# The conv branch's input projection as 2x2 block products: seven products of half size in place of eight, in two groups of 1024 tokens

## Chip, core and metric

The kernel runs on one core of a Trainium2 chip. The metric is device microseconds of one execution. In three runs the kernel before took 3139.97, 3140.99 and 3141.83 us, median 3140.99 us.

## What is computed

A two-layer decoder trunk on 2048 tokens of width 1024, in float32. The layer that the change touches projects the normed input to eight parts, runs retention on four of them and a gated short convolution on the other four, and projects both results back:

```python
q, k, v, g_ret, cb, cc, cx, g_conv = split_cols(h @ w_in, EVEN_SPLITS)
...
y_conv = cb * short_conv(cc * cx, conv_w, conv_b)
mix = jnp.concatenate([r * jax.nn.silu(g_ret), y_conv * jax.nn.silu(g_conv)], axis=-1)
return mix @ w_out
```

`cb`, `cc`, `cx` and `g_conv` are each 2048 tokens by 1024 channels, so the conv branch's input projection is 1024 x 4096 weights against 1024 x 2048 inputs. The convolution has three taps along the tokens. The second layer (latent attention) is not touched.

## The kernel before

**Numbers.** PE multiplies in fp32r. Each float32 operand is kept as a high part (a ScalarE copy) and a low part (VectorE: source less high part), by `split` (L72 to 74), and each product is three matmuls, high x high, high x low, low x high (`mm3`, L76 to 79). The transposed input lies in `uTH[tb]`, `uTL[tb]`, four blocks of 512 tokens.

**Retention (L284 to 498).** 64 units (8 heads, 8 pairs of 128 tokens) run as a software pipeline in which step `s` projects unit `s` on PE (48 matmuls), rotates and gates it (`post`), and finishes units `s-1` to `s-3`. PE passes through these pieces in the order in which they are written; so does every other engine through its own. Three more steps drain the pipeline; in them PE already runs the first convolution product (`conv_mm(0, ...)`, L478), while GpSimd, VectorE and ScalarE finish the last units.

**Convolution (L500 to 535).** For each of 8 blocks of 128 channels the parts cx, cc, g_conv, cb follow each other. One part is 128 channels x 2048 tokens: two calls of `conv_mm`, each 2 x 8 x 3 = 48 matmuls of 128x128 against 128x512 into a PSUM tile of two banks (tag `proj`, two buffers), 3072 matmuls in all. Behind PE each bank is read once: cx is copied by ScalarE, cc multiplied by VectorE, then two taps by VectorE, and so on. Weights come as raw pieces by SyncE's queue and are split by `piece_split`, 64 pieces.

**Order and memory.** Nothing schedules: the order is that of the code, engine by engine, and a semaphore stands where one engine needs another's result. Tiles come from pools, and a new tile in a place waits for every reader and writer of the tile before it there; dependences are followed by tile (`reuse_waits="tile"`), so two banks in one tile count as one. The weight tiles are a ring of three (tag `w`, L172). The output side (L537 on) opens new pools over the same memory; its first three weight tiles (`worw`, L616) lie where the third tile of that ring lay.

## Time and profile before

| | |
|---|---|
| median of 3 runs | 3140.99 us |
| span of the profiled execution | 3139.9 us |
| retention and everything ahead of it | 0 to 719.6 us |
| convolution products on PE | 719.6 to 1420.4 us |
| output side and second layer | 1421.8 us on |
| busy share: PE, VectorE, ScalarE, GpSimd | 99%, 43%, 32%, 17% |

The page covers one execution; its own time is its span, 3139.9 us, from the first instruction to the last, and what lies around it in a run is the 1.1 us to the median. A matmul's listed duration (389 ns in the convolution) is its way through the array and overlaps with the next one's, so rates are read from counts in a stretch, not from durations.

### The profile page before, as it was taken

How to read it: one execution, taken by the hardware profiler on the slowest of the kernel's cores; microseconds unless marked ns; L12 is line 12 of the kernel's file. 1: busy time of each engine (PE TensorE's matmuls, PEld its weight loads, DVE VectorE, ACT ScalarE, POOL GpSimd, SP SyncE). 2: the span in 40 equal slices, each digit the busy share in tenths (PEclk: the TensorE clock that was granted, in tenths of full speed). 3: DMA queues.
4: the chain of work that ended last, by engine and by line, in shares of the span. 5: the costliest groups of instructions: out<-in, count | busy, mean ns of one | idle time of the engine just before them, and what ended most of it. 6: DMA issues, size and time to landing. Idle time of an engine off the chain costs nothing.

```text
span 3139.9 us, 44468 instructions
## 1 busy us (share of the span) xinstructions
PE 3105.7 (99%) x17169; PEld 2739.2 (87%) x17169; DVE 1361.8 (43%) x3102; ACT 996.3 (32%) x2593; POOL 547.7 (17%) x941
## 2 busy tenths in 40 slices
PE   7999999999999999999999999999999999999998
PEld 7999999998888888888888888998899999999887
DVE  6533333332211222225323311568666666666643
ACT  5322122211111111114222321343555555555521
POOL 2111111110000000000111101014333333333210
PEclk9999999999999999999999999999999999999999
DMA  4210111001111111116333532325312211112552
GB/s 137 63 32 29 35 35 31 25 31 31 37 38 37 41 38 37 30 38 210 121 118 111 176 126 78 115 91 214 109 61 63 71 51 60 58 57 62 170 164 85
DMA packets 226325, 244.64 MB, mean 78 GB/s; under 512 B 33841, under 2 KB 189121, under 8 KB 226113
## 3 DMA queue, kind: packets, MB, share of 16 engines
q1 hardware_dynamic: 201360, 158.13, 16.9%
q0 software_dynamic: 24432, 83.38, 7.1%
q8 instruction: 135, 2.21, 0.3%
q14 instruction: 78, 0.63, 0.1%
q10 hardware_dynamic: 320, 0.29, 0.0%
HBM read 157.86 MB, written 83.89 MB: 77 GB/s over the span
## 4 chain that ended last, share of the span: by engine, by line
PE 97%; DVE 1%; DMA 1%; ACT 1%; issue 0%; SPq 0%; POOL 0%; DVEq 0%; POOLq 0%; ACTq 0%
PE y L582 11%; PE cv L77 7%; PE cv L79 7%; PE cv L78 7%; PE pj L77 6%; PE pj L79 6%; PE pj L78 6%; PE fy L1354 5%; PE T L1159 4%; PE o L1189 2%; PE o L1188 2%; PE o L1187 2%; PE S L1106 2%; PE S L1109 2%; PE S L1110 2%; PE S L1107 2%
## 5 line engine op out<-in xcount | busy, mean ns | idle before, releaser
L77 PE MATMUL cv<-uTH,w_c 128*128 128x512 f32 x1024 | 398.6, 389 | 1.4 <-ACT p L517 1.4
L79 PE MATMUL cv<-uTH,w_c 128*128 128x512 f32 x1024 | 398.4, 389 | 0.0
L78 PE MATMUL cv<-uTL,w_c 128*128 128x512 f32 x1024 | 398.4, 389 | 0.0
L77 PE MATMUL pj<-w_r,uTH 128*128 128x384 f32 x896 | 310.5, 346 | 0.0
L79 PE MATMUL pj<-w_r,uTL 128*128 128x384 f32 x896 | 299.9, 335 | 0.0
L78 PE MATMUL pj<-w_r,uTH 128*128 128x384 f32 x896 | 299.6, 334 | 0.0
L1127 POOL TENSOR_SCALAR P<-P,al 128x512 f32<-128x512 f32 (+2 forms) x320 | 218.7, 694 | 354.5 <-DVE al L1132 169.4
L1117 ACT ACTIVATE P<-S,nm 128x512 f32<-128x512 f32 (+2 forms) x320 | 200.8, 628 | 197.7 <-DVE nm L1114 172.4
L77 PEld LDWEIGHTS cv<-uTH,w_c 128*128 128x128 f32 x1024 | 192.2, 188 | 41.5 <-ACT p L517 1.7
L79 PEld LDWEIGHTS cv<-uTH,w_c 128*128 128x128 f32 x1024 | 192.2, 188 | 40.0
L78 PEld LDWEIGHTS cv<-uTL,w_c 128*128 128x128 f32 x1024 | 192.2, 188 | 39.8
L1114 DVE TENSOR_REDUCE nm<-S 128x1 f32<-128x512 f32 (+2 forms) x320 | 194.4, 609 | 71.3 <-PE S L1110 43.1
L1187 PE MATMUL o<-TH,vH 128*128 128x256 f32 x576 | 185.2, 322 | 0.0
L1163 DVE TENSOR_TENSOR TL<-T,TH 128x512 fp32r<-128x512 f32 x224 | 154.3, 689 | 63.3 <-ACT TH L1162 62.0
L77 PEld LDWEIGHTS pj<-w_r,uTH 128*128 128x128 f32 x896 | 168.3, 188 | 9.6 <-issue 9.6
L78 PEld LDWEIGHTS pj<-w_r,uTH 128*128 128x128 f32 x896 | 168.5, 188 | 0.0
L79 PEld LDWEIGHTS pj<-w_r,uTL 128*128 128x128 f32 x896 | 168.2, 188 | 0.0
L1159 PE MATMUL T<-ident,P 128*128 128x128 f32 x1088 | 166.2, 273 | 0.0
L1189 PE MATMUL o<-TH,vL 128*128 128x256 f32 x576 | 162.9, 283 | 0.0
L1188 PE MATMUL o<-TL,vH 128*128 128x256 f32 x576 | 162.2, 282 | 0.0
L582 PE MATMUL y<-woH,mH 128*128 128x512 f32 x512 | 159.0, 392 | 1.4 <-ACT woH L73 1.4
L582 PE MATMUL y<-woH,mL 128*128 128x512 f32 x512 | 157.7, 389 | 0.1
(310 smaller groups left out, 6691.6 us busy)
## 6 DMA issues: line engine op xcount, KB each, us to landing
raw<-in_even_w_in SPq DMA_DIRECT2D x94, 256.0 KB, 3.0
qn_d<-qn POOLq DMA_DIRECT2D x32, 512.0 KB, 3.1
aqn<-qn_d SPq DMA_DIRECT2D x64, 256.0 KB, 3.2
mr<-mix_d SPq DMA_DIRECT2D x56, 256.0 KB, 2.8
mix_d<-mxo POOLq DMA_DIRECT2D x32, 256.0 KB, 2.7
mix_d<-a POOLq DMA_DIRECT2D x16, 512.0 KB, 3.5
worw<-in_even_w_out SPq DMA_DIRECT2D x16, 512.0 KB, 5.0
xr<-in_x SPq DMA_DIRECT2D x16, 512.0 KB, 4.0
```

The source lines that it names most:

```text
L77: PE.matmul(o, ah, bh, start=first, stop=False)
L78: PE.matmul(o, ah, bl, start=False, stop=False)
L79: PE.matmul(o, al, bh, start=False, stop=last)
L582: PE.matmul(ys[t][i], a, w[k][:, i * 512:(i + 1) * 512], start=first and pi == 0, stop=last and pi == 2)
L1114: V.reduce_max(nm[:, j:j + 1], sp[:, 0:w], axis=AX.X, negate=True)
L1117: later(D_EXP, lambda: A.activation(p_[:, 0:w], sp[:, 0:w], AF.Exp, bias=nm[:, j:j + 1], accum_out=sm[:, j:j + 1]))
L1127: G.tensor_scalar(t_[:, 0:ww], t_[:, 0:ww], al[:, jj:jj + 1] if n > 1 else al[:, 5:6], al[:, 5:6] if n > 1 else 1.0, op0=ALU.mult, op1=ALU ...
L1159: PE.transpose(tp[:, e, z, :], src, ident)
L1187: PE.matmul(hold[i], vH[h][:, kb, :], pth[:, c], start=first, stop=False)
L1188: PE.matmul(hold[i], vH[h][:, kb, :], ptl[:, c], start=False, stop=False)
L1189: PE.matmul(hold[i], vL[h][:, kb, :], pth[:, c], start=False, stop=last)
L1354: PE.matmul(y[i], a[:, k, :], w[k][:, i * 512:(i + 1) * 512], start=k == 0 and pi == 0, stop=k == KT - 1 and pi == 2)
```

## The change

The conv projection is taken as a 2x2 block product. A *quad* is one block of 128 channels in two of the four parts (even quads: cx and cc; odd quads: g_conv and cb), both halves of the 1024 input rows (4 weight blocks A11, A12, A21, A22, each 512 rows by 128 channels), and two token blocks of 512 (4 input blocks B11 to B22). There are 32 quads: two groups of 1024 tokens, in each 8 channel blocks, in each an even and an odd quad. In place of eight block products a quad has seven, of 12 matmuls each, in the order A11, S2, S1, S3, A22, A12, S4; S1 to S4 are sums and differences of weight blocks, and each is multiplied by its partner B11, T2, T1, T3, T4, B21, B22, where T1 to T4 are sums and differences of input blocks. The four results are put together from PSUM by further sums: `p1_copy` (ScalarE copies the A11 product), `u2_`, `u3`, `c22`, `c21`, `c12` (VectorE). S3 adds onto the bank of S2, A12 onto that of A11, S4 onto that of S1, so each of these has to wait until VectorE or ScalarE has read what stood there.

The T blocks are made once by GpSimd during retention (`comb_ops`, three instructions a step from step 10 on, 108 additions of 128x512), written to memory, and read back and split when their group needs them (`u_dma`, `u_split_`). The S blocks are made by GpSimd per quad (`w_step`, 5 additions of 128x512), and all seven weight blocks are split per quad, one quad ahead of PE; as each weight block is used in both groups, its data is loaded and split twice. Products A11, S2, S1 of the first quad fill the drain of retention. What follows the sums (`finish`) is put off until after the next quad's first product. The vector `gnb` gives way to one per head, and its place is used for sums (`tc`).

```diff
+    uc_d = dram.tile([2, 7, P, 4, 512], F32, name="uc_d")
...
+        ORDER = ("A11", "S2", "S1", "S3", "A22", "A12", "S4")
+        UOF = dict(zip(ORDER, ("B11", "T2", "T1", "T3", "T4", "B21", "B22")))
+        UIX = {n_: i for i, n_ in enumerate(("B11", "T2", "T1", "T3", "T4", "B21", "B22"))}
+        BANK = dict(zip(ORDER, (0, 1, 2, 1, 3, 0, 2)))
+        QUADS = [(g, ct, w) for g in range(2) for ct in range(8) for w in range(2)]
+        COFF = ((OCX, OCC), (OGC, OCB))
...
+        def w_step():
+            n_ = wcnt["prep"]
+            q, j = divmod(n_, 7)
+            if q >= len(QUADS):
+                return
+            wcnt["prep"] += 1
+            i = ORDER[j]
+            r = qraw[q]
+            f = lambda t: t.rearrange("p k c -> p (k c)")
+            if j == 0:
+                r["s"] = base.tile([P, 2, 4, P], F32, tag="tc", bufs=1, name=f"s12_{q}")
+                r["S1"], r["S2"] = r["s"][:, 0], r["s"][:, 1]
+                G.tensor_tensor(out=r["S1"], in0=r["A21"], in1=r["A22"], op=ALU.add)
+                G.tensor_tensor(out=r["S2"], in0=r["S1"], in1=r["A11"], op=ALU.subtract)
+            elif j == 3:
+                r["s"] = base.tile([P, 2, 4, P], F32, tag="tc", bufs=1, name=f"s34_{q}")
+                r["S3"], r["S4"] = r["s"][:, 0], r["s"][:, 1]
+                G.tensor_tensor(out=r["S3"], in0=r["A11"], in1=r["A21"], op=ALU.subtract)
+                G.tensor_tensor(out=r["S4"], in0=r["A12"], in1=r["A22"], op=ALU.subtract)
+                G.tensor_tensor(out=r["S4"], in0=r["S4"], in1=r["S3"], op=ALU.add)
+            if n_ % 3 == 0:
+                wring.append(w_tile(f"wq{n_}"))
+            t = wring[-1][:, (n_ % 3) * 1024:(n_ % 3 + 1) * 1024].rearrange("p (z k c) -> p z k c", z=2, k=4)
+            split(t[:, 0], t[:, 1], r[i])
+            qtile[q, i] = t
+            if j == 5:
+                raw_dma()
+        def banks(q):
+            if q not in bks:
+                if q % 2 == 0:
+                    t_ = [psb.tile([P, 2, 512], F32, tag="proj", bufs=2, name=f"qb{q}_{i}") for i in range(2)]
+                    bks[q] = [t_[0][:, 0, :], t_[1][:, 0, :], t_[0][:, 1, :], t_[1][:, 1, :]]
+                else:
+                    bks[q] = [psb.tile([P, 512], F32, tag=tg, bufs=1, name=f"qb{q}_{tg}") for tg in ("tr", "m", "sc", "r")]
+            return bks[q]
+        def p1_copy(q):
+            p1[q] = base.tile([P, 512], F32, tag="p1", bufs=1, name=f"p1_{q}")
+            A.copy(p1[q], banks(q)[0])
+        def product(q, i):
+            b = BANK[i]
+            o = banks(q)[b]
+            W, (UH, UL) = qtile.pop((q, i)), ucs[QUADS[q][0]][UOF[i]]
+            for k in range(4):
+                first = k == 0 and i in ("A11", "S2", "S1", "A22")
+                mm3(o, W[:, 0, k, :], W[:, 1, k, :], UH[:, k, :], UL[:, k, :], first, k == 3, i in ("A12", "S3", "S4"))
+        def u_dma(g, n_, tag, where=None):
+            if where is None:
+                t = base.tile([P, 2, 4, 512], F32R, tag=tag, name=f"uc{g}_{n_}")
+                where = (t[:, 0], t[:, 1])
+            ucs[g][n_] = where
+            SP.dma_start(f32(where[1]), uc_d[g, UIX[n_]])
+        def u_split_(g, n_):
+            H, L = ucs[g][n_]
+            for c in (slice(0, 2), slice(2, 4)):
+                A.copy(H[:, c], f32(L)[:, c])
+                V.tensor_tensor(out=L[:, c], in0=f32(L)[:, c], in1=f32(H)[:, c], op=ALU.subtract)
+        UTAG = {"T2": "uTH2", "T1": "uTL2", "T3": "uTH3", "T4": "uTL3", "B21": "uTH0", "B22": "uTL0"}
...
+        NG = len(QUADS) // 2
+        USPLIT = {(NG - 1, 0): "B11", (NG - 1, 5): "T2", (NG - 1, 6): "T1", (NG, 1): "T3", (NG, 2): "T4", (NG, 3): "B21", (NG, 4): "B22"}
...
+                    def first(H=H, L=L, g=g, k=k):
+                        t = base.tile([P, 2, 512], F32, tag="tc", bufs=1, name=f"tc12_{g}{k}")
+                        c0, c1 = t[:, 0], t[:, 1]
+                        yield lambda: sub(c0, H("B12"), H("B11"))
+                        yield lambda: sub(c1, L("B12"), L("B11"))
+                        yield lambda: add(c0, c0, c1)
+                        yield lambda: sub(c1, H("B22"), c0)
+                        yield lambda: add(c1, c1, L("B22"))
+                        yield lambda: (put("T1", c0), put("T2", c1))
...
-                if n <= s < n + 2:
-                    conv_mm(0, s - n)
+                if s == n:
+                    product(0, "A11")
+                    product(0, "S2")
+                elif s == n + 1:
+                    p1_copy(0)
+                    product(0, "S1")
...
+                if s > 9:
+                    for _ in range(3):
+                        f_ = next(tops, None)
+                        if f_ is not None:
+                            f_()
+                if s == n - 7:
+                    raw_dma()
+                for _ in range({n - 6: 1, n - 5: 1, n - 4: 1, n: 2, n + 1: 2}.get(s, 0)):
+                    w_step()
+                if s == n - 3:
+                    u_dma(0, "T2", UTAG["T2"])
+                    u_dma(0, "T1", UTAG["T1"])
...
+                elif s == n - 2:
+                    u_split_(0, "T2")
+                elif s == n - 1:
+                    u_split_(0, "T1")
+                    u_dma(0, "T3", UTAG["T3"])
+                    u_dma(0, "T4", UTAG["T4"])
+                elif s == n + 1:
+                    u_split_(0, "T3")
+                elif s == n + 2:
+                    u_split_(0, "T4")
...
+            for q, (g, ct, w) in enumerate(QUADS):
...
+                for j, i in enumerate(ORDER):
+                    if q > 0 or i not in done0:
+                        product(q, i)
+                    if last:
+                        u_next(j)
+                    if j == 0:
+                        flush()
+                    elif j == 1:
+                        if q > 0:
+                            p1_copy(q)
+                    elif j == 2:
+                        u2_ = cp.tile([P, 512], F32, tag="u2", bufs=1, name=f"u2_{q}")
+                        V.tensor_tensor(out=u2_, in0=x_, in1=p1[q], op=ALU.add)
+                    elif j == 4:
+                        u3 = p1.pop(q)
+                        V.tensor_tensor(out=u3, in0=x_, in1=u3, op=ALU.add)
+                        c22 = cp.tile([P, 512], F32, tag="c", bufs=4, name=f"c22_{q}")
+                        V.tensor_tensor(out=c22, in0=y_, in1=u3, op=ALU.add)
+                    elif j == 5:
+                        c21 = cp.tile([P, 512], F32, tag="c", bufs=4, name=f"c21_{q}")
+                        V.tensor_tensor(out=c21, in0=u3, in1=z_, op=ALU.subtract)
+                    w_step()
+                    if (q, j) in USPLIT:
+                        u_split_(1, USPLIT[q, j])
+                def finish(q=q, g=g, ct=ct, w=w, a=a, y_=y_, u2_=u2_, c21=c21, c22=c22, pv=pv, av=av):
+                    c12 = cp.tile([P, 512], F32, tag="c", bufs=4, name=f"c12_{q}")
+                    if w == 0:
+                        V.tensor_tensor(out=pv[:, 2:514], in0=a, in1=c21, op=ALU.mult)
+                        V.tensor_tensor(out=c12, in0=y_, in1=u2_, op=ALU.add)
+                        G.tensor_copy(pv[:, 0:2], halo[:, ct, :])
+                        V.tensor_tensor(out=pv[:, 514:1026], in0=c12, in1=c22, op=ALU.mult)
+                        for o in (0, 512):
                             A.activation(av[:, o:o + 512], pv[:, 2 + o:2 + o + 512], AF.Identity, scale=convw[:, 2, ct:ct + 1],
                                          bias=convb[:, ct:ct + 1])
+                        for o in (0, 512):
                             for tap in (1, 0):
                                 V.scalar_tensor_tensor(out=av[:, o:o + 512], in0=pv[:, tap + o:tap + o + 512],
                                                        scalar=convw[:, tap, ct:ct + 1], in1=av[:, o:o + 512],
                                                        op0=ALU.mult, op1=ALU.add)
...
+                        if g == 0:
+                            G.tensor_copy(halo[:, ct, :], pv[:, 1024:1026])
+                    else:
+                        sa = cp.tile([P, 512], F32, tag="c", bufs=4, name=f"sa_{q}")
+                        A.activation(sa, a, AF.Silu)
+                        V.tensor_tensor(out=c12, in0=y_, in1=u2_, op=ALU.add)
+                        A.activation(c12, c12, AF.Silu)
+                        V.tensor_tensor(out=av[:, 0:512], in0=c21, in1=av[:, 0:512], op=ALU.mult)
+                        V.tensor_tensor(out=av[:, 0:512], in0=sa, in1=av[:, 0:512], op=ALU.mult)
+                        V.tensor_tensor(out=av[:, 512:1024], in0=c22, in1=av[:, 512:1024], op=ALU.mult)
+                        V.tensor_tensor(out=av[:, 512:1024], in0=c12, in1=av[:, 512:1024], op=ALU.mult)
+                        o = g * 1024
+                        G.dma_start(mix_d[D + ct * P:D + (ct + 1) * P, o:o + 1024], av)
+                late.append(finish)
+            flush()
```

On PE, in an even quad (number 2) and in the odd one behind it, products have these heads and waits; `qb_0` and `qb_1` are the even quad's two tiles of two banks each, `qb_tr`, `qb_m`, `qb_sc`, `qb_r` the odd quad's single banks, and `cv_0` the tile of two banks before. Before, from one part to the next:

```order
L79 MATMUL cv_1_7645<-uTH_858,w_c_7408 128x512
L77 MATMUL cv_0_7706<-uTH_172,w_c_7523 128x512 [waits DVE_49]
L78 MATMUL cv_0_7706<-uTL_173,w_c_7523 128x512
...
L77 MATMUL cv_0_7706<-uTH_172,w_c_7523 128x512 [waits Activation_49]
...
L77 MATMUL cv_1_7766<-uTH_602,w_c_7523 128x512 [waits DVE_49]
```

Now, S3, A22, A12 and S4 of the even quad, then A12 and S4 of the odd one:

```order
L78 MATMUL qb_1_7025<-uc_T_6660,wq_6931 128x512 [waits DVE_49]
...
L78 MATMUL qb_1_7025<-uc_T_6662,wq_6983 128x512
...
L78 MATMUL qb_0_7024<-uTH_174,wq_6983 128x512 [waits DVE_49]
...
L78 MATMUL qb_0_7024<-uTH_373,wq_6983 128x512
...
L78 MATMUL qb_tr<-uTH_174,wq_7104 128x512 [waits Activation_49]
...
L78 MATMUL qb_sc<-uTH_373,wq_7160 128x512 [waits DVE_49]
```

Before, a product of 24 matmuls goes to a fresh bank and waits at most for an old reader. Now a quad waits for VectorE inside itself: at S3 in both kinds, and then at A12 in the even quad but at S4 in the odd one.

On VectorE in the steady state, before, a part of cc and the weights behind it (`a_`, `p_` the convolution's buffers, `w_c` weights):

```order
L519 TENSOR_TENSOR p_8407<-cv_0_8521,p_8407 128x512 [waits PE_49]
L523 SCALAR_TENSOR_TENSOR a_8408<-p_8407,convw,a_8408 128x512 [waits Activation_49]
L523 SCALAR_TENSOR_TENSOR a_8408<-p_8407,convw,a_8408 128x512 [waits DVE_49]
L74 TENSOR_TENSOR w_c_8578<-raw_8349,w_c_8578 128x512 [waits DMAHW7_49,Activation_49]
L519 TENSOR_TENSOR p_8407<-cv_1_8583,p_8407 128x512 [waits PE_49]
```

And now, in the odd quad 3, from the last taps of quad 2 to `c21` (`wq` weights, `s_` S blocks made by GpSimd, `p_3` the copy of the A11 product and then `u3`, `c_3` first `c22` and then `c21`):

```order
L718 SCALAR_TENSOR_TENSOR a_7027<-p_7026,convw,a_7027 128x512 [waits DVE_49]
L74 TENSOR_TENSOR wq_7160<-qA_4_7144,wq_7160 128x512 [waits DMAHW2_49,Activation_49]
L74 TENSOR_TENSOR wq_7160<-s_4_7191,wq_7160 128x512 [waits Activation_49]
L693 TENSOR_TENSOR u_3_7224<-qb_m,p_3_7208 128x512 [waits PE_49]
L74 TENSOR_TENSOR wq_7226<-s_4_7191,wq_7226 128x512 [waits Activation_49]
L74 TENSOR_TENSOR wq_7226<-s_4_7241,wq_7226 128x512 [waits Activation_49]
L696 TENSOR_TENSOR p_3_7208<-qb_m,p_3_7208 128x512 [waits DVE_49,PE_49]
L698 TENSOR_TENSOR c_3_7260<-qb_sc,p_3_7208 128x512 [waits DVE_49]
L74 TENSOR_TENSOR wq_7226<-qA_4_7142,wq_7226 128x512 [waits DMAHW1_49,Activation_49]
L701 TENSOR_TENSOR c_3_7276<-p_3_7208,qb_r 128x512 [waits PE_49]
```

What PE waits for (`u2_`, `u3`, `c22`) now stands behind the taps of the quad before and behind weights of the quad to come, two of which come from GpSimd.

On SyncE, at the end of the convolution, `raw` and `qA` being weight pieces and `worw`, `mr` the output side's inputs. Before:

```order
L264 DMA raw_9699<-in_even_w_in 128x4x128 [waits DMAHW2_49,DVE_49]
L264 DMA raw_9756<-in_even_w_in 128x4x128 [waits DMAHW3_49,DVE_49]
L264 DMA raw_9812<-in_even_w_in 128x4x128 [waits DMAHW4_49,DVE_49]
L617 DMA worw_10274<-in_even_w_out 128x1024 [waits PE_49]
L618 DMA mr_0_10273<-mix_d 128x256 [waits DMASW0_49,Pool_49]
```

Now:

```order
L297 DMA qA_31_10939<-in_even_w_in 128x4x128 [waits DMAHW1_49,DVE_49]
L297 DMA qA_31_10941<-in_even_w_in 128x4x128 [waits DMAHW0_49,DVE_49,Pool_49]
L297 DMA qA_31_10943<-in_even_w_in 128x4x128 [waits DMAHW2_49,DVE_49]
L818 DMA worw_11225<-in_even_w_out 128x1024 [waits DVE_49,PE_49]
L819 DMA mr_0_11224<-mix_d 128x256 [waits DMASW0_49,Pool_49]
```

The order is the same. The wait of `worw` is on whatever last used its place: before, the weights of part 29, which PE left two parts ahead of the end; now ring tile 74 (`wq222`), which holds the weights of the last quad's last two products, A12 and S4.

## Rows read from the trace of the kernel before

**Rows 1.** Page: busy time by engine, and the chain that ended last.

```profile
PE 3105.7 (99%) x17169; PEld 2739.2 (87%) x17169; DVE 1361.8 (43%) x3102; ACT 996.3 (32%) x2593; POOL 547.7 (17%) x941
...
PE 97%; DVE 1%; DMA 1%; ACT 1%; issue 0%; SPq 0%; POOL 0%; DVEq 0%; POOLq 0%; ACTq 0%
```

**Rows 2.** Busy by stretch: length, PE, PEld, DVE, ACT, POOL, clock, DMA.

```profile
300.00:600.00 300.00, 300.00 (x1857) 284.67 (x1858) 113.96 (x355) 61.90 (x245) 49.52 (x74) 1.00 0.11 32
...
900.00:1160.00 260.00, 260.00 (x1149) 215.28 (x1148) 55.16 (x84) 35.08 (x60) 3.26 (x9) 1.00 0.13 37
```

**Rows 3.** Tile of the convolution products: count, ns min/median/max, first and last start.

```profile
L77 PE MATMUL cv<-uTH,w_c x1024: 389/389/501, 719.6 to 1419.5; 128*128 128x512 f32 x171
```

**Rows 4.** VectorE by line: count | busy us, mean ns | idle before, releaser.

```profile
L523 DVE SCALAR_TENSOR_TENSOR a<-p,convw,a 128x512 f32<-128x512 f32 x64 | 48.1, 752 | 30.0 <-ACT a L520 28.8
...
L74 DVE TENSOR_TENSOR w_c<-raw,w_c 128x512 fp32r<-128x512 f32 x64 | 44.1, 690 | 162.8 <-ACT w_c L73 162.8
...
L527 DVE TENSOR_TENSOR a<-cv,a 128x512 f32<-128x512 f32 x32 | 20.6, 686 | 140.0 <-PE cv L79 140.0
...
L74 DVE TENSOR_TENSOR ut<-ur,ut 128x1024 fp32r<-128x1024 f32 x16 | 19.5, 1220 | 37.9 <-ACT ut L73 37.8
```

**Rows 5.** ScalarE by line.

```profile
L73 ACT CAST w_c<-raw 128x512 fp32r<-128x512 f32 x64 | 38.2, 622 | 3.5 <-PE pj L79 3.5
...
L520 ACT ACTIVATE a<-p,convb,convw 128x512 f32<-128x512 f32 x32 | 26.1, 817 | 167.7 <-DVE p L519 167.7
...
L517 ACT COPY p<-cv 128x512 f32<-128x512 f32 x32 | 17.3, 593 | 275.1 <-PE cv L79 275.1
...
L73 ACT CAST ut<-ur 128x1024 fp32r<-128x1024 f32 x16 | 16.8, 1049 | 0.8 <-DMA ur<-u2t_d 0.8
```

**Rows 6.** GpSimd by line.

```profile
L111 POOL TENSOR_TENSOR rss<-rss,nhalf 128x2 f32<-128x2 f32 x64 | 44.7, 699 | 179.9 <-DVE rss L110 178.3
...
L534 POOL DMA_DIRECT2D mix_d<-a x16 | 8.5, 532 | 667.8 <-DVE a L527 667.8
```

**Rows 7.** GpSimd in time, 10 to 26 us: start, length, instruction, idle before.

```profile
11.87 1.05 POOL L142 TENSOR_TENSOR scr<-rt_b 128x512 f32<-128x512 f32 x1
13.00 1.47 POOL L145 TENSOR_SCALAR scr<-scr 128x512 f32<-128x512 f32 x1
14.55 1.81 POOL L146 TENSOR_SCALAR scr<-scr 128x512 f32<-128x512 f32 x1
```

**Rows 8.** VectorE in time, the same stretch.

```profile
11.93 2.06 DVE L210 SCALAR_TENSOR_TENSOR xs_uTH<-xs_uTH,ss,gpre 128x1024 f32<-128x1024 f32 x1 [2.16 <-POOL ss L206]
13.92 2.11 DVE L74 TENSOR_TENSOR w<-raw,w 128x512 fp32r<-128x512 f32 x2
...
19.54 1.28 DVE L74 TENSOR_TENSOR w<-ws__96,w 128x512 fp32r<-128x512 f32 x2
21.29 1.28 DVE L210 SCALAR_TENSOR_TENSOR xs_uTH<-xs_uTH,ss,gpre 128x1024 f32<-128x1024 f32 x1 [0.46 <-POOL ss L206]
```

**Rows 9.** VectorE in time, around the last retention unit.

```profile
706.22 0.42 DVE L334 TENSOR_TENSOR t<-pj,cosT 128x256 f32<-128x256 f32 x1 [1.53 <-PE pj L79]
...
716.89 0.42 DVE L334 TENSOR_TENSOR t<-pj,cosT 128x256 f32<-128x256 f32 x1 [0.26 <-PE pj L79]
...
718.53 0.28 DVE L383 SCALAR_TENSOR_TENSOR stt<-stt,kv 64x128 f32<-64x128 f32 x1
```

**Rows 10.** PE in time, first product of the output side.

```profile
1421.80 1.20 PE L582 MATMUL y<-woH,mH 128*128 128x512 f32 x4 [1.44 <-ACT woH L73]
```

**Rows 11.** SyncE in time, its first issue for the output side.

```profile
1376.88 0.34 SPq L617 DMA_DIRECT2D worw<-in_even_w_out  x1
```

**Rows 12.** DMA issues: size of each, median us from issue to landing.

```profile
worw<-in_even_w_out SPq DMA_DIRECT2D x16, 512.0 KB, 5.0
```

**Rows 13.** PE in time, after its waits at the start.

```profile
19.56 0.52 PE L79 MATMUL pj<-w,uTL 128*128 128x384 f32 x1
...
22.74 0.34 PE L77 MATMUL pj<-w,uTH 128*128 128x384 f32 x1
```

More of the change, by code (lines that the diff above doesn't have):

```diff
@@ L74, in split, with mm3 @@
         sub.tensor_tensor(out=l, in0=src, in1=f32(h), op=ALU.subtract)
[L76 to L79 removed]
+    def mm3(o, ah, al, bh, bl, first, last, again=False):
+        kw = dict(skip_group_check=True) if again else {}
+        PE.matmul(o, ah, bh, start=first, stop=False, **kw)
+        PE.matmul(o, ah, bl, start=False, stop=False, **kw)
+        PE.matmul(o, al, bh, start=False, stop=last, **kw)
     def bc(ap, shape):
@@ L231, in x_tr_all @@
             xn.clear()
-        CSEQ = [(ct, ty) for ct in range(8) for ty in range(4)]
-        COFF = (OCX, OCC, OGC, OCB)
         pieces = []
```

143 lines of the change are left out of this document (85 added, 58 removed).

## Prediction

> **What bounds the kernel now.** I read the page first: PE is busy for 3105.7 of 3139.9 us, and the chain that ended last is PE for 97% [rows 1]. Then the stretches: in 900 to 1160 us, all convolution, PE runs 1149 matmuls in 260.00 us, 226.3 ns each, at full granted clock and without a gap, while VectorE is busy 55 us, ScalarE 35 and GpSimd 3 [rows 2]. The products last from 719.6 us [rows 3] to 1420.4, where the next stage's first matmul is at 1421.80 behind 1.44 us of waiting [rows 10]. So this stage is bound by the number of its matmuls, and only PE's own waits can eat a saving there. Then, by line, what the changed stage is built of.
>
> **Removed.** Eight products of a quad become seven: 384 of 3072 matmuls go, of an unchanged shape. 384 x 226.3 ns = **-86.9 us**. No weight load comes on top: a load goes with each matmul as before.
>
> **Added inside a quad.** T is the end of a quad's predecessor on PE; a product takes 12 x 226.3 ns = 2.72 us, so S3 could start at T+8.15, A22 ends at 13.58. VectorE takes 0.69 us for 128x512, 0.75 for a tap, 1.22 for 128x1024 [rows 4]; ScalarE 0.62, 0.82 for the tap with the bias, 0.59 for a copy, 1.05 for 128x1024 [rows 5]. In a chain VectorE work costs slightly less each (two in 1.28 us [rows 8]). GpSimd's addition of 128x512 has one near row, 1.05 us; the slowest row of that size is 1.81 [rows 7]. I take 1.1, since that row is the operation itself, and keep 1.05 to 1.81.
>
> *Even quad, A12.* Its four banks are two tiles. `u3` reads the tile of S3 and A22, so it waits for A22 too, and A12 writes the tile from which `c22` still reads, so PE waits for `u3` and `c22`: 2 x 0.69 and the handing over, 1.45 us. PE has nothing else in its order. In the odd quad each bank is its own tile, `c22` is wanted only at S4, and A12's 2.72 us hide it. 16 x 1.45 = **+23.2 us**, which I hold for the surest of the added terms (0.7 to 1.7 each).
>
> *Even quad, S3.* It waits for `u2_`, which stands on VectorE behind the odd predecessor's `finish`, two weight splits, and by way of them GpSimd. `finish`: `c12` after T, four multiplications, T+3.3. GpSimd's store behind it, 0.53 [rows 6], with the handing over some 0.85 (an estimate): T+4.15. S1 and S2 at 1.1 each, behind the store in its order: T+6.35. ScalarE's copy 0.62, VectorE's 0.69, `u2_` 0.69: T+8.5. PE waits 0.4 us; with 1.81 per addition T+9.9, 1.7. 15 quads (the first is in the start below): **+6 us** (0 to 25).
>
> *Odd quad, S3.* `finish` of the even predecessor: two products and a sum, T+2.05; four taps, T+5.05; two splits, `u2_`: T+7.1. S1 and S2 are ready by T+4.6. That is in time by 1 us, if GpSimd and VectorE do not hinder each other. The trace says that they do: from 11.87 to 16.36 us GpSimd's three instructions took 4.33 us [rows 7], and VectorE's beside them 2.06 and 2.11 where the same take 1.28 alone [rows 8]. If the 2.2 us of S1 and S2 add to the taps fully, `u2_` ends at T+9.3 and PE waits 1.15. I take 0.5, 16 x 0.5 = **+8 us** (0 to 21).
>
> The Trainium skill has a rule for that, in "SBUF — State Buffer", section "Who interferes with whom": a VectorE instruction with two inputs in SBUF contends with a GpSimd instruction that reads SBUF, and one of the two blocks. The trace agrees, with the 2.06 against 1.28 us just named. By the rule in full the odd quad pays 1.15 us, the stage 18 us in place of 8; by no contention, none.
>
> GpSimd's S3 and S4, ring places and the reloaded weights have a whole product or more of slack. VectorE's load is some 16 to 18 instructions or 11 to 12.5 us in a quad of 19 us, ScalarE's under 7: neither becomes the bound by itself.
>
> **Added once.** *Start.* The last unit's projection ends at 716.9 [rows 9]. Before, VectorE is then done with it by 718.8, and PE has 21.8 us of convolution (96 matmuls) with which to cover the drain. Now it has three products, 8.15 us, and the drain has more in it. VectorE's order is: T1 split (2.4), the drained units (about 2 us twice, each with 0.70 of GpSimd [rows 6]), four weight splits, T3 and T4 split (2.4 each), two weight splits, `u2_`. From the score product behind S2, at 726.0: 0.7, 1.3, unit 63 with its wait for ScalarE and GpSimd to 729.85, 1.3, 4.7, 1.3, 0.7, together 737.8. PE, which started A11 at 719.9, is free for S3 at 730.2 without waits. **+8 us** (3 to 12, by how much of the splits overlaps the drain).
>
> *Change of groups, quads 15 and 16.* Seven T and B blocks are split, 2.4 us each on VectorE, their places free only as each product of quad 15 ends. T3's split stands ahead of `u2_` of quad 16: T+11.8 instead of 8.5, so 3.3 us more; B21's stands ahead of `u3` there and T4's ahead of A22, some 0.4, and B11's ahead of `u2_` of quad 15, 0.2. **+4 us** (2 to 8).
>
> *End.* SyncE's first output weight was issued at 1376.88 [rows 11], 43.5 us ahead of the end, because its place was free after part 29. Its place now belongs to S4 of the last quad, PE's very last product; nothing can be prefetched, and the first `mr` is queued behind it on SyncE. So from the last matmul: issue, 5.0 us to landing [rows 12], 1.05 us of ScalarE, some 6.15 in place of 1.44. **+4.7 us** (3.5 to 8). What follows streams as before, since `worw` 3 and on wait for a split in both.
>
> *Retention.* 108 additions on GpSimd, three a step: 3.3 us in a step of 10.67 (from one unit's rotation to the next [rows 9]), where GpSimd is busy 49.5 of 300 us, or 17% [rows 2]. They stand ahead of the reciprocal root that VectorE waits for. VectorE has 1.53 us of idle time ahead of its next rotation [rows 9], and the transposes need the rotated unit only half a step later; that is the cover, and I cost it at 0. Without it: 1 us in each of the 44 steps.
>
> **Sum.** -86.9 + 23.2 + 6 + 8 + 8 + 4 + 4.7 = -33.0. 3139.9 - 33.0 = 3106.9 us for a profiled span; the median of the runs lies 1.1 above the span, so **3108 us**, 1.05% less than before.
>
> **A price left out.** PE idles some 6 us in a row at start and end. After waits of 2 to 5 us at the kernel's start its matmuls of 384 columns took 0.52 us, ten of them 3.18 us, and later 0.34 [rows 13]. Should that come back, about 1.6 us for each gap, inside the range. "TensorE: Matmul & The Clock Gate" of the Trainium skill, part 1, holds that an idle array falls to 1.2 GHz and has to be warmed up by work; by it the sum would be 3111.
>
> **Rivals.**
> 1. *The waits are hidden.* If VectorE and GpSimd run slightly faster than I chain them, S3 never waits (terms 6 and 8 gone) and the one-time terms are at their lower ends (8.5 in place of 16.7): 3108 - 14 - 8.2 = 3086. For it: 1 us of slack in the odd quad, and VectorE at 21% in the stage before. Against it: the A12 wait stays in any case, and the contention row.
> 2. *GpSimd sets the pace.* If an addition costs 1.81 us under contention, the even quad waits 1.7, and in the odd one S1 and S2 beside the taps put `u2_` at T+10.7, 2.5: 15 x 1.3 + 16 x 2.0 more, 3108 + 51.5 = 3159, **slower**. It decides from about 2 us per pair of quads over my terms, 1.55 us per addition. For it: 1.47 and 1.81 are what GpSimd took beside VectorE [rows 7]. Against: those have other operations, and the addition beside a 2.06 us VectorE instruction took 1.05.
> 3. *Retention is stretched.* A late reciprocal root delays `post`, which delays PE's transposes: 44 steps x 1 us: 3152, slower. Against it: GpSimd's 17%.
> 4. *The stage pays everything but these two*, all single terms near their upper ends: 3125 to 3135, a bare gain.
>
> **Chances.** My case (3092 to 3125) 0.64; rival 1 (below 3092) 0.14; rival 4 0.08; rival 2 0.09, of which a third stays below 3135; rival 3 0.05. Faster and slower begin 0.2% off the median, at 3134.7 and 3147.3, about what a measurement can tell. Faster is my case, rivals 1 and 4 and that third, 0.88 rounded down; of what is left somewhat under half ends between the bounds, so same 0.05, slower 0.07. The range for 8 in 10 leaves out half of rival 1 and the slower ends: 3086 to 3136; my case alone is 3092 to 3125.
>
> **What would show it.** The matmul rate in the middle of the stage still 226 ns inside a product. In even quads a PE wait of 1.4 us ahead of A12, released by VectorE's `c22`, 16 times; no such wait in odd quads. Ahead of S3 waits under 1 us, released by `u2_`. A gap of some 6 us ahead of the first quad's S3, and one of some 6 us between the last product and the output side, released by a DMA. GpSimd's additions at about 1.1 us. Retention's end still near 717 us. I am wrong if even quads run without the A12 wait, if the additions take 1.5 us or more, or if retention ends later.

## The result, and the profile after

The changed kernel takes 3165.22 us (median of 4 runs, 3160.83 to 3165.82), the kernel before 3141.19 (4 runs): ratio **1.0073**, 95% interval 1.0059 to 1.0087. It is slower by 0.7%; the forecast was 3108, faster. The profiled execution took 3164.7 us, with a span of 3162.9, 23.0 above the 3139.9 of before.

The page of after, busy time by engine and then the chain that ended last, answers to [rows 1]:

```profile
PE 3049.7 (96%) x16785; PEld 2678.4 (85%) x16785; DVE 1635.8 (52%) x3444; ACT 1110.9 (35%) x2775; POOL 917.1 (29%) x1226
...
PE 81%; issue 6%; DVE 6%; POOL 3%; DMA 1%; ACT 1%; SPq 0%; POOLq 0%; DVEq 0%; ACTq 0%
```

384 matmuls are gone, 17,169 to 16,785, and PE is busy 56 us less. But its share fell from 99 to 96%: the chain that ended last now runs through VectorE and GpSimd for 9%, where VectorE had 1% of it and GpSimd none. The same by stretch (columns as in [rows 2]):

```profile
720.00:760.00 40.00, 28.28 (x119) 22.33 (x118) 26.70 (x37) 15.43 (x33) 15.78 (x16) 0.87 0.30 101
760.00:1060.00 300.00, 271.58 (x1152) 217.63 (x1151) 171.47 (x233) 79.33 (x136) 103.69 (x90) 0.98 0.21 65
1060.00:1130.00 70.00, 56.61 (x214) 44.96 (x213) 51.61 (x60) 29.31 (x41) 20.59 (x16) 0.88 0.38 131
...
1180.00:1430.00 250.00, 230.32 (x1000) 186.19 (x999) 135.72 (x199) 67.77 (x116) 78.67 (x67) 1.00 0.19 57
```

Before, 260 us held 260.00 of PE. Now 300 us in the middle of the stage hold 271.58, with VectorE at 57% and GpSimd at 35%: neither is full, yet PE waits. At the start and at the change of groups (first and third row) the granted clock is 0.87 and 0.88 besides. What PE waits for (engine, line, what it waited for: total us, times, longest):

```profile
PE qb L78 <- DVE u L693: 31.8, 16, 9.0
PE qb L78 <- DVE c L698: 25.7, 16, 3.1
PE qb_m L78 <- DVE u L693: 15.2, 10, 4.4
...
PE y L783 <- ACT woH L73: 5.8, 1, 5.8
...
PE qb L78 <- ACT p L339: 4.3, 2, 3.1
```

`u` is `u2_`, ahead of S3: the first row is the even quads (their banks are `qb`), the third those odd ones that wait. `c` L698 is `c22`, ahead of A12 in even quads. `y` is the end, `p` is `p1` ahead of S1, at the start and at the change of groups.

**The books.** In what follows, the wait ahead of a product is the start of its first matmul less that of PE's matmul before it, less 226.3 ns. "Inside" is what the product's other eleven starts lose against 226.3 ns each. The S3 waits of 2.44 and 2.33 us come back every third quad; the experiment with one more weight place (`e12_ring4`) shows why.

| term | forecast | measured |
|---|---|---|
| 384 matmuls removed, 226.3 ns each | -86.9 | -86.9 |
| A12, even quads, 16 x 1.67 | +23.2 | +26.7 |
| S3, even quads 2 to 30 but 16: nine at 1.12, five at 2.44 | +6 | +22.3 |
| S3, odd quads but 15: five at 1.0, two at 2.33, two at 1.28, six at 0 | +8 | +12.2 |
| start: S3 9.06, S1 1.24 | +8 | +10.3 |
| quads 15 and 16: 4.6, 3.2, 3.0, and 1.55 more at A12 | +4 | +12.4 |
| end: 6.14 from start to start, 1.83 before | +4.7 | +4.3 |
| retention: first product at 719.59, before 719.59 | 0 | 0 |
| inside products | 0 | +22.6 |
| before's own waits and losses in the stage, gone | 0 | -2.8 |
| behind the stage's end | 0 | +1.3 |
| sum | -33.0 | +22.4, and the spans differ by 23.0 (waits of 0.2 us and less make up the rest) |

**An even quad.** Quad 4 on VectorE, GpSimd and ScalarE; its first product starts at 819.97 on PE, which is T:

```profile
820.17 0.69 DVE L726 TENSOR_TENSOR c<-qb_sc,u 128x512 f32<-128x512 f32 x1 [0.73 <-PE qb_sc L80]
...
822.97 0.69 DVE L731 TENSOR_TENSOR a<-c,a 128x512 f32<-128x512 f32 x1
823.58 0.68 DVE L74 TENSOR_TENSOR wq<-qA,wq 128x512 fp32r<-128x512 f32 x1
827.91 0.69 DVE L74 TENSOR_TENSOR wq<-s,wq 128x512 fp32r<-128x512 f32 x1 [3.65 <-ACT wq L73]
828.52 0.68 DVE L693 TENSOR_TENSOR u<-qb,p 128x512 f32<-128x512 f32 x1
...
823.96 0.57 POOL L733 DMA_DIRECT2D mix_d<-a  x1 [10.14 <-DVE a L731]
824.55 1.31 POOL L312 TENSOR_TENSOR s<-qA,qA 128x512 f32<-128x512 f32 x1
825.93 1.29 POOL L313 TENSOR_TENSOR s<-s,qA 128x512 f32<-128x512 f32 x1
...
827.25 1.14 ACT L73 CAST wq<-s 128x512 fp32r<-128x512 f32 x2 [3.78 <-POOL s L313]
```

The chain is the one forecast, each link a little longer: `finish` ends at T+3.7 (forecast 3.3), the store at T+4.6 (4.15), S1 and S2 at T+7.25 (6.35), `u2_` at T+9.2 (8.5). VectorE stands idle for 3.65 us between, at the split of S2 (of the quad that is being prepared), which waits for GpSimd's sum and stands ahead of `u2_`.

**The additions by line** (as in [rows 6]); S1, S2, the parts of S4, and one line of the T sums in retention:

```profile
L319 POOL TENSOR_TENSOR s<-s 128x512 f32<-128x512 f32 x32 | 48.5, 1515 | 2.5
...
L313 POOL TENSOR_TENSOR s<-s,qA 128x512 f32<-128x512 f32 x32 | 45.4, 1419 | 2.6 <-DMA qA<-in_even_w_in 0.2
...
L312 POOL TENSOR_TENSOR s<-qA,qA 128x512 f32<-128x512 f32 x32 | 42.0, 1311 | 51.5 <-DVE wq L74 51.2
...
L383 POOL TENSOR_TENSOR tc<-tc,uTL 128x512 f32<-128x512 f32 x16 | 21.0, 1312 | 0.9
```

1.3 us, where 1.1 was taken from the 1.05 of [rows 7]. That row is not the operation itself, as the prediction has it: it multiplies two operands of 16 and 32 numbers that are repeated along the tile (L142 of the kernel before). The trace of before has a nearer row, with one input repeated only twice, at half the width:

```profile
L345 POOL TENSOR_TENSOR sg<-sg,gnb 128x256 f32<-128x256 f32 x64 | 47.3, 738 | 219.1 <-ACT sg L343 219.1
```

The additions of half width below (`e8_half`) take 0.74 to 0.76 us, as this row does.

**Inside.** PE behind its longest wait, at the first S3 (start, length, idle before):

```profile
740.95 0.77 PE L78 MATMUL qb<-uc_T,wq 128*128 128x512 f32 x1 [9.02 <-DVE u L693]
741.51 0.63 PE L79 MATMUL qb<-uc_T,wq 128*128 128x512 f32 x1
741.94 0.63 PE L80 MATMUL qb<-uc_T,wq 128*128 128x512 f32 x1
```

And the stretch of this product (columns as in [rows 2]):

```profile
740.95:746.20 5.25, 5.25 (x12) 4.14 (x13) 1.55 (x2) 1.14 (x2) 4.24 (x4) 0.50 0.35 103
```

Behind the first, the matmuls start 0.427 us apart: the granted clock is 0.50 there, that is 1.2 GHz. Of twelve waits of 2.33 us and more in the stage, nine are followed by this, and cost 1.5 to 2.3 us more inside the product, 16.3 in all; after the other three (quads 3, 24 and 30) and after shorter waits it does not show in this execution. Thirty-five waits of 1 to 2.4 us without it lose some 0.14 each at the restart, 4.9 in all.

**The end.** SyncE's first output weight, then PE (answers to [rows 10, 11]):

```profile
1437.86 0.34 SPq L818 DMA_DIRECT2D worw<-in_even_w_out  x1
...
1443.58 2.07 PE L783 MATMUL y<-woH,mH 128*128 128x512 f32 x4 [5.75 <-ACT woH L73]
```

Issued behind the last product and not 43 us ahead; the four matmuls take 2.07 us where they took 1.20 in [rows 10]: the clock again.

### The profile page after: what moved, and what is told of

Read it like the earlier page. It is cut to its first block, busy times and chain, and to the rows that moved or that the text cites. A ratio compares the mean times of both kernels' runs of the same rounds, so it can differ in the third digit from the quotient of the medians.

```text
span 3162.9 us, 45037 instructions
## 1 busy us (share of the span) xinstructions
PE 3049.7 (96%) x16785; PEld 2678.4 (85%) x16785; DVE 1635.8 (52%) x3444; ACT 1110.9 (35%) x2775; POOL 917.1 (29%) x1226
## 4 chain that ended last, share of the span: by engine, by line
PE 81%; issue 6%; DVE 6%; POOL 3%; DMA 1%; ACT 1%; SPq 0%; POOLq 0%; DVEq 0%; ACTq 0%
PE y L783 11%; PE pj L78 6%; PE pj L80 5%; PE pj L79 5%; PE fy L1555 5%; PE T L1360 4%; PE o L1390 2%; PE o L1389 2%; PE o L1388 2%; PE qb L78 2%; PE S L1307 2%; PE S L1310 2%; PE S L1311 2%; PE S L1308 2%; PE S L1309 2%
## 5 line engine op out<-in xcount | busy, mean ns | idle before, releaser
L74 DVE TENSOR_TENSOR wq<-s,wq 128x512 fp32r<-128x512 f32 x128 | 103.0, 804 | 177.2 <-ACT wq L73 176.9
L73 ACT CAST wq<-s 128x512 fp32r<-128x512 f32 x128 | 76.9, 619 | 274.4 <-POOL s L313 72.4
L783 PE MATMUL y<-woL,mH 128*128 128x512 f32 x512 | 158.4, 391 | 0.0
L78 PE MATMUL qb<-uc_T,wq 128*128 128x512 f32 x256 | 106.3, 415 | 36.1 <-DVE u L693 31.8
L1363 ACT CAST TH<-T 128x512 fp32r<-128x512 f32 x224 | 131.0, 585 | 24.0 <-PE T L1360 18.7
L1360 PEld LDWEIGHTS T<-ident,P 128*128 128x128 f32 x1088 | 125.4, 141 | 7.7
```

What stands on the lines that cost most here:

```text
L78: PE.matmul(o, ah, bh, start=first, stop=False, **kw)
L783: PE.matmul(ys[t][i], a, w[k][:, i * 512:(i + 1) * 512], start=first and pi == 0, stop=last and pi == 2)
L1360: PE.transpose(tp[:, e, z, :], src, ident)
```

## The experiments

All spans are set against 3162.9 of after unless another kernel is named. The single edits ran once each, the combinations four times. The four runs of after lie within 5.0 us, so where a span moves by less than that, only the waits in the trace tell anything.

**Banks paired otherwise** (`e1_bank`): the bank of A11 and A12 now shares its tile with that of S2 and S3, and the bank of S1 and S4, which `c22` reads, with that of A22.

```diff
-  bks[q] = [t_[0][:, 0, :], t_[1][:, 0, :], t_[0][:, 1, :], t_[1][:, 1, :]]
+  bks[q] = [t_[0][:, 0, :], t_[0][:, 1, :], t_[1][:, 0, :], t_[1][:, 1, :]]
```

> Only the even quad's banks are paired differently: A11/A12's bank with S2/S3's in one tile, S1/S4's with A22's in the other, so that u3 no longer waits for A22 and A12 no longer for c22. Theory A (each wait of PE has its own cause in the order): the 16 waits ahead of A12, 1.67 us each by the changed kernel's trace, go and nothing takes their place, with the restart behind each some 27 to 31 us less, a span of 3132 to 3136 against 3162.9. Rival B (VectorE's and GpSimd's chains set the pace of a quad anyway): the time comes back ahead of S3 or S4, a gain under 10 us.

Span 3133.2, -29.7. The row of `c` L698 is gone from the waits, and A12's 28.3 us have become 2.5:

```profile
PE qb L78 <- DVE u L693: 38.8, 16, 9.4
PE qb_m L78 <- DVE u L693: 12.2, 10, 4.5
```

7 us went over to S3 of even quads, most of it in quad 16, whose S3 now waits 8.2 us in place of 3.0; S3 of odd quads lost 3.0, and inside, 22.6 fell to 16.9. So the expected span came out, though not with nothing in the waits' place. The wait was the tile's, as forecast.

**S1 and S2 ahead of finish** (`e2_pool`): they are added on GpSimd after the last weight split of the quad ahead.

```diff
+                    if j == 6:
+                        s12(q + 2)       # S1, S2 of the quad prepared next
                     if (q, j) in USPLIT:
```

> Only the place of GpSimd's S1 and S2 additions changes: they are issued behind the last weight split of the quad before, ahead of that quad's finish with its store or halo copy. Theory A (S3 waits because these additions stand behind the store and the halo copy on GpSimd): the S3 waits of the steady quads, 22 us in the even and 12 us in the odd ones of the changed kernel, fall to under 8 together, the half-clock stretches that follow the 2.4 us waits go too, 26 to 40 us less, span 3123 to 3137. Rival B (the additions contend with VectorE wherever they stand, so the taps and the products of finish end later): S3 waits stay above 0.8 us in most quads, gain under 10 us.

Span 3123.9, -39.0. S3 of even quads 34.3 to 12.3 (9.1 of it is quad 0), of odd quads 16.8 to 10.5 (3.9 is quad 15), inside 22.6 to 11.1:

```profile
PE qb L78 <- DVE c L704: 27.2, 16, 4.6
PE qb L78 <- DVE u L699: 11.3, 7, 9.0
PE qb_m L78 <- DVE u L699: 9.7, 5, 3.8
```

So the place of the additions in GpSimd's order, behind the store and the halo copy and so behind `finish`, is what S3 waited for, and the largest single loss.

**The start** (`e3_start`): `u2_` of quad 0 ahead of T4's split and two weight splits.

> Only in the first quad u2_ is put ahead of the T4 split and of two weight splits on VectorE. Theory A: the wait ahead of the first S3, 9.1 us, falls by the 2.4 + 1.3 us now behind u2_, with the half-clock stretch after it shortened: 4 to 6 us less, span 3157 to 3159. Rival: the T3 split or its data come as late as that anyway, no change within 1 us, or A22 waits for T4 instead.

Span 3159.4, -3.5, slightly under what was expected, and within what single runs differ by. The wait is clear: S3's fell from 9.06 to 4.53, by more than the 3.7 named, and A12 waited 0.4 longer.

**The output weights early, first form** (`e4_end`): their places lie in the pool kept through both stages.

```diff
-            wr_[k] = cp.tile([P, D], F32, tag="wraw", bufs=3, name=f"worw{k}")
+            wr_[k] = mid.tile([P, D], F32, tag="u2", bufs=3, name=f"worw{k}")
```

> Only the output side's weight tiles worw take other places (those of a tile that is used later), which the convolution frees 5 us or more ahead of its end. Theory A: the first three are loaded ahead again, the gap between the last product and the output side falls from 5.8 us of waiting to about 1.4, and the half-clock stretch behind it goes: 4 to 6 us less, span 3157 to 3159. Rival: the first mr, still queued on SyncE, holds the stage up as long, no change within 1 us.

Missed: span 3173.1, **+10.2**. The end did what was expected, with 2.69 us of waiting in place of 5.75; then a wait came up 370 us later that after does not have, and with what follows on it 13.4 us were lost there (10.2 and the 3.2 by which the output side starts sooner):

```profile
PE gt L78 <- ACT u_1t L73: 9.6, 1, 9.6
```

**The same, second form** (`e5_end2`): only the first three weights are moved, the others stay.

> The changed kernel with the first three output weights of the next stage in places of the pool that is kept through both stages (so that nothing of the convolution holds them), the later ones where they were, so that the pool's layout stays. Theory A (the end's 4.3 us come from the first output weights' place belonging to the last product): the gap between the last product and the next stage's first matmul goes from 6.1 us to 1.8 to 3.1, no new wait appears in the gate projection, and the span goes from 3162.9 to 3157 to 3160. Rival B (the gap is set by the last evacuations and a bank anyway): the gap stays above 5 us and the span within 1 us of 3162.9.

Missed again: span 3165.3, +2.3, with the same 9.6 us ahead of `gt`. My reason, that the old pool had lost a tag, was too coarse. What the next pool's first loads wait for in the program shows the rest: places are laid out in the order of the first claim, so the mixed rows now came first, and the loads of `u2r` lay over rows and weights that the output stage's last products still read. SyncE in this run:

```profile
1775.85 22.11 SPq L869 DMA_DIRECT2D u2r<-u2t_d  x4
```

The gate projection's weights stand in the same queue behind these loads. The span hides some of the loss, since the convolution, whose code is that of after, ended 7.3 us sooner here (see the end of the experiments).

**Third form** (`e9_end3`): the places of weights 3 to 5 are claimed first.

```diff
+            if k == 0:
+                wr3.extend(cp.tile([P, D], F32, tag="wraw", bufs=3, ...) for i in range(3))
```

> As the run before with the first three output weights in the kept pool, but the places of the later weights are claimed first, so that the next pool's loads lie over the weights again, which are free early, and not over the mixed rows, which the last products of the output stage still read. Theory A: the gap at the end stays at about 3.1 us, the 9.6 us ahead of the gate projection are gone, and the span is 3153 to 3158. Rival B (the gate projection is late because its predecessor starts sooner): the 9 us stay, and the span stays at 3163 to 3166.

Span 3157.8, -5.2; no wait ahead of `gt`, 2.69 at the end. SyncE passes three of the loads at once:

```profile
1781.81 1.56 SPq L876 DMA_DIRECT2D u2r<-u2t_d  x3
```

The layout was the cause. The gap at the end, from start to start, falls from 6.14 to 3.08, so the place of the first weights accounts for 3.1 of the 4.3 us of the end; 1.3 of the 5.2 fell in the convolution, which this edit does not touch.

**Half additions** (`e8_half`): S1 and S2 over 256 of 512 columns, the rest set to zero.

> The changed kernel with S1 and S2 added over half their columns (the other half is set to zero, which changes the output), so each GpSimd addition takes some 0.7 us in place of 1.3 to 1.6, and a fill of some 0.5 us stands beside them. Theory A (the additions' length sets when even quads' S3 starts): the median wait ahead of S3 in even quads goes from 1.1 us to under 0.3, that of quads behind a ring wait from 2.4 to about 1.2, and the span falls by 12 to 25 us. Rival B (VectorE's chain of finish, splits and u2_ is late by itself): the wait of even quads stays at 0.9 us or more, and the span falls by less than 6 us.

Span 3133.0, -29.9, more than expected: S3 of odd quads gains too (16.8 to 7.5), and inside, 22.6 fell to 15.2. GpSimd in the even quad 4 (beside the rows of after above):

```profile
821.34 0.76 POOL L312 TENSOR_TENSOR s<-qA,qA 128x256 f32<-128x256 f32 x1
822.02 0.54 POOL L313 MEMSET s<- 128x512 f32 x1
822.50 0.74 POOL L314 TENSOR_TENSOR s<-s,qA 128x256 f32<-128x256 f32 x1
```

From the start of S1 to the end of S2 it is 1.90 us, 2.67 before: 0.77 shorter; and the wait ahead of S3 fell from 1.12 to 0.35, by 0.77. In quads behind a ring wait (`e12_ring4` below) it fell from 2.44 to 1.68, not to the 1.2 expected, by the same 0.76. In even quads the wait follows GpSimd one to one.

**The halo copy** (`e11_halo`) on ScalarE, behind its two taps.

```diff
-                            G.tensor_copy(halo[:, ct, :], pv[:, 1024:1026])
+                            A.copy(halo[:, ct, :], pv[:, 1024:1026])
```

> The changed kernel with the halo's copy-out (2 columns, group 0 only) on ScalarE behind its two taps in place of GpSimd ahead of S1. Theory A (GpSimd waits at the halo copy for VectorE's multiplication and so starts S1 late): the median wait ahead of S3 in odd quads of group 0 falls from 1.0 us to under 0.4, as group 1 has it, and the span falls by 4 to 12 us. Rival B (VectorE's four taps, stretched beside GpSimd, set u2_): the median stays at 0.8 us or more, the span within 3 us.

Span 3150.3, -12.6, just past the upper end. Odd quads of group 0 no longer wait, but for quads 3 and 9, which go from 2.33 to 1.29, as group 1 has it, and 15, at the change of groups (4.60 to 3.56). Quad 5 of after, VectorE and GpSimd:

```profile
844.24 5.08 DVE L718 SCALAR_TENSOR_TENSOR a<-p,convw,a 128x512 f32<-128x512 f32 x4
...
844.46 0.58 POOL L722 COPY halo<-p 128x2 f32<-128x2 f32 x1 [10.14 <-DVE p L712]
844.99 1.29 POOL L312 TENSOR_TENSOR s<-qA,qA 128x512 f32<-128x512 f32 x1
846.36 1.63 POOL L313 TENSOR_TENSOR s<-s,qA 128x512 f32<-128x512 f32 x1
```

And with the copy on ScalarE:

```profile
842.31 2.98 DVE L718 SCALAR_TENSOR_TENSOR a<-p,convw,a 128x512 f32<-128x512 f32 x4
...
837.02 1.29 POOL L312 TENSOR_TENSOR s<-qA,qA 128x512 f32<-128x512 f32 x1 [4.63 <-DVE wq L74]
838.39 1.29 POOL L313 TENSOR_TENSOR s<-s,qA 128x512 f32<-128x512 f32 x1
```

GpSimd had been idle for 10.14 us and stood at a copy of two columns that waits for VectorE. Without it the additions are done by 839.7, before `finish` begins at 840.4; with it they run beside the four taps, which then take 5.08 us in place of 2.98.

**One more weight place** (`e12_ring4`). Three weight products share a tile, and there are three tiles; every third quad the first product of a new tile (an S4) has to wait for the end of the quad ahead. Here that product has its own place.

```diff
+            own = n_ % 3 == 0 and j == 6 and "cp" in box
-            if n_ % 3 == 0:
+            if n_ % 3 == 0 and not own or box.pop("next", False):
                 wring.append(w_tile(f"wq{n_}"))
+            if own:
+                t = box["cp"].tile([P, 1024], F32R, tag="w4", bufs=1, ...)
```

> The changed kernel with one more place for a weight product: the S4 product whose split had to wait, in every third quad, for the end of the quad ahead gets a place of its own (the room for it comes from two small tiles laid over a mask that is no longer read). Theory A (that wait stands ahead of finish on ScalarE and VectorE): the waits ahead of S3 in even quads 6, 12, 18, 24 and 30 fall from 2.4 to 1.1 us, in odd 3 and 9 from 2.3 to 1.0, in 21 and 27 from 1.3 to 0; 9 x 1.3 = 12 us, and what the clock lost behind gaps of 2.3 us or more comes on top: the span falls by 10 to 24 us. Rival B (some other thing repeats every third quad): unchanged within 3 us.

Span 3142.5, -20.4. S3 waits 1.13 in quads 6, 12, 18, 24 and 30, 1.00 and 0.99 in 3 and 9, nothing in 21 and 27: each as expected. In after, quad 6 (T is 862.3: S3's start at 872.88 less 2.44 and 8.15) had this on VectorE:

```profile
863.21 0.69 DVE L74 TENSOR_TENSOR wq<-s,wq 128x512 fp32r<-128x512 f32 x1 [3.75 <-ACT wq L73]
863.82 0.68 DVE L726 TENSOR_TENSOR c<-qb_sc,u 128x512 f32<-128x512 f32 x1
```

The split, held by ScalarE and that by PE, stands ahead of `finish`, which begins at T+1.5. With the added place `finish` comes first, at T+0.2 (T is 860.71 there):

```profile
860.91 0.69 DVE L734 TENSOR_TENSOR c<-qb_sc,u 128x512 f32<-128x512 f32 x1 [2.42 <-PE qb_sc L80]
```

**Together** (`e6_comb`): banks as in `e1_bank` (A12 does share a tile with S3; what it no longer shares is the bank that `c22` reads), early S1 and S2, start, and the end in its second form.

> Four edits together: banks paired so that A12 shares no tile with S3 and A22; S1 and S2 of a quad formed before the finish of the quad ahead of it; T4's split behind u2_ at the start; the first three output weights loaded early. Theory A (each removes its own wait and they don't hide one another): the gains seen singly, 29.7 + 39.0 + 3.5 + about 4, come to 76, so a span of 3085 to 3095 from 3162.9, and 1.4 to 1.8% less time than the kernel before. Rival B (VectorE's order alone sets the pace, so a wait removed comes back at the next product): not under 3110.

3109.23 us, ratio to before 0.9894 (0.9878 to 0.9911), span 3108.1: under the 3110 of the rival, but 13 us above the expected range and 21 short of the sum of 76. Inside the stage the gains nearly add up: its last matmul starts at 1370.65, 66.8 earlier than in after, against 72.2 singly. What is left is mostly behind the stage, where 15.0 us are lost, 9.5 of them the wait ahead of `gt`.

**Two more** (`e7_comb2`): taps and halo copy behind `u2_` of the next quad; the seven splits spread over quads 14 to 16.

```diff
+  USPLIT = {(NG-2, 4): "B11", (NG-1, 4): "T2", (NG-1, 5): "T1", (NG-1, 6): "T3", (NG, 2): "T4", ...}
   V.tensor_tensor(out=u2_, in0=x_, in1=p1[q], op=ALU.add)
+  for f in late2:        # the taps and the halo copy of the quad ahead
+      f()
```

> The four edits, and two more: the four taps and the halo copy stand behind u2_ of the quad after, and the seven splits at the change of groups are spread over quads 14 to 16. Theory A (what is left in odd quads is VectorE's taps ahead of u2_ beside GpSimd, and at the change the splits): a further 4 to 15 us less than the four edits alone. Rival B (the taps only change places, and are late for the quad that needs av): within 3 us of the four edits, or slower.

3097.3 us, 0.9859 (0.9844 to 0.9874), 13.1 less by span. No odd quad waits any more. The two edits were not run apart.

**With the third form of the end** (`e10_comb3`), the best version (the "second form" of the expectation is the one called third here):

> The six edits with the end in this second form. Theory A: as the six edits (3095.0) less the 9.5 us ahead of the gate projection, a span of 3084 to 3088, and 1.7 to 1.9% less time than the kernel before. Rival B: within 2 us of 3095.

**3083.07 us, ratio 0.9815 (0.9799 to 0.9831)**, span 3081.4: faster than both kernels, and 2.6 us under the lower end expected. What PE still waits for in the stage:

```profile
PE qb L78 <- DVE u L708: 6.6, 6, 4.9
PE qb L78 <- ACT uc_T L365: 4.6, 1, 4.6
...
PE y L803 <- ACT woH L73: 2.7, 1, 2.7
PE qb L78 <- DVE c L719: 2.5, 2, 1.3
```

And its middle, 278.19 of 280 us on PE (260.00 of 260 before the change), at full granted clock, with VectorE at 64%:

```profile
760.00:1040.00 280.00, 278.19 (x1217) 227.32 (x1216) 178.16 (x250) 89.54 (x149) 107.75 (x94) 1.00 0.27 85
```

**The same waits, another clock.** After and the three runs with the end alone (`e4_end`, `e5_end2`, `e9_end3`) have the same convolution code, and their waits come to nearly the same, 84.3, 84.8, 84.9 and 85.3 us. Inside the products they lost 22.6, 22.7, 15.2 and 20.3, as nine, nine, four and eight of twelve long waits were followed by half clock. S3 of quad 6, behind 2.44 us of waiting in after and 2.45 in e5; first its first matmuls in after:

```profile
872.88:875.60 2.72, 2.72 (x6) 2.14 (x7) 0.62 (x2) 0.73 (x2) 2.04 (x2) 0.50 0.03 6
```

And the whole product in e5:

```profile
872.07:874.80 2.73, 2.73 (x12) 2.25 (x13) 0.61 (x2) 0.72 (x2) 2.04 (x2) 1.00 0.03 6
```

From the stage's first matmul to its last it is 717.8 us in after and 711.0 in e5: 6.8 us less with five half-clock stretches fewer. This is the clock's price with the waits kept. It also says how far single spans can be trusted: 7 of the 22.6 us come and go between executions of the same code.

## Why the prediction was wrong, step by step

*Right.* The gain (-86.9: the nominal time of the stage fell by just that, and e10 gets 58 us of it). The A12 wait in even quads and its cause (1.67 us for 1.45; e1). No such wait in odd quads. The end, 4.3 for 4.7, and its cause (e9 takes back 3.1 of it). Retention untouched, so rival 3 falls. The signs of all terms.

*Failed most: "A price left out".* It named the clock behind a gap, gave it two gaps of 1.6 us, and kept it out of the sum. The unit price was good (1.5 to 2.3 us), the count was not: nine gaps in the stage, 16.3 us, and with the restarts 22.6 inside products, the largest of the misses. The nine are the start, the four waits at the change of groups and four of the seven S3 waits behind the ring, most of them longer than the sum had them, so these terms pay twice. The four runs with the same convolution code show the price with the waits kept; where the runs took long waits away, half-clock stretches behind them went too: inside 22.6 in after, 11.1 in e2, 9.5 in e10. "TensorE: Matmul & The Clock Gate" of the Trainium skill, part 1, gives idling as the cause; the rows above, 0.63 us behind 9.02 of idling, agree, and the sum should have held it.

*Mis-sized: "Even quad, S3", 6 against 22.3.* The chain was right, its links too short by 0.7 us together: an addition 1.3 in place of 1.1, `finish` 0.4 longer. (The links as the prediction lists them end at T+8.35; 0.15 of its 8.5 stands in no term.) For a wait that is the small rest of a sum of nine links (8.5 against 8.15), 0.7 us is not 8% but three times the wait. e8 shows the additions' share, one to one; e2 that the chain as a whole was the cost.

*False: "ring places ... have a whole product or more of slack".* In every third quad they have none: 9 x 1.3 = 11.8 us of the S3 terms (6.6 even, 5.2 odd; e12), so 6.6 of the 22.3 above are this step's.

*Half right: "Odd quad, S3", 8 against 12.2.* S1 and S2 were said to be ready by T+4.6. They would be ready before T, but for the halo copy, an instruction of 0.58 us that I costed at nothing; it moves them onto the taps. There VectorE and GpSimd hinder each other: the four taps take 5.08 us in place of 2.98 beside additions of 1.29 and 1.63. The Trainium skill's "SBUF — State Buffer", section "Who interferes with whom", has a VectorE instruction with two inputs in SBUF contend with a GpSimd instruction that reads SBUF, by an exclusive lock. The trace agrees in kind, though the taps lost only 2.10 us to additions of 2.92. With the additions counted onto the taps in full I had 1.15 us a quad; group 0 shows 1.0, group 1, with no halo copy-out, 0. I took a mean of two cases that are both real, each in its half (e11). The ring waits above are the rest of the term.

*Mis-sized: the change of groups, 4 (2 to 8) against 12.4.* Of that some 2 are the waits of a regular quad. Its stalls were costed one by one; on VectorE they stand in one queue. With the splits spread and the taps moved (e7), quad 15 no longer waits, while quad 16's S3 keeps 4.8.

*The start, 8 against 10.3,* inside its 3 to 12.

*The rivals.* Rival 2 named the right engine for the S3 waits, priced 3159 at 1.81 us per addition, and was held to decide from 1.55 on. The additions took 1.31 to 1.52 by line, so by its own bound it does not decide; and the whole of the S3 terms is 34.5 us here, not the 65.5 that it needs. Rival 4, all single terms near their upper ends, 0.08, is nearest to what happened, but without the clock, the ring and the change of groups its 3135 falls short by 30. The terms were treated as independent. They hang on one chain (VectorE's `finish`, GpSimd's additions, the splits), and were all late together; added up, the upper ends that the prediction itself names (27.2, 25, 21, 12, 8 and 8) come to 3155, and the range should have reached there. Of the signs of being wrong that the prediction named, none came clearly (one line of additions passed 1.5 us by a little), though it was wrong: the signs watched the A12 wait, the additions and retention. That S3 waits stay under 1 us stood only among what would show it right, and 1.12 and 2.44 answer it.

*Open.* Why some of the long waits show no half clock. It does not go by the place in the code: quad 3's wait of 2.33 us is followed by it in e9 and not in after, quad 18's of 2.44 in after and not in e9.

## What to carry to other kernels

When a change trades matmuls for work on other engines, list for each helper what stands ahead of it in its engine's order and what that waits for. Here a store's issue of 0.57 us and a copy of two columns of 0.58 us, each waiting for VectorE, held back 2.6 us of additions; moving the additions ahead of both gained 39 us by the spans, moving the copy alone 12.6. A wait worked out as the difference of two long sums needs the error of the sums for its range, and waits on one chain are late together. The seven-product form was not the loss: with these waits taken away by another order and other places, and no arithmetic removed, 3165 became 3083, where the kernel before takes 3141.
